# Mixture-of-experts stage of a two-layer trunk: wider weight pieces, a third extra buffer, and another path for the emptier experts

## The chip, the cores and the metric

The kernel runs on one core of a Trainium2 chip, in one launch. The metric is the device time in microseconds (us), the median of several executions. Engines are named as the profile names them: PE is TensorE, PEld its weight load, DVE VectorE, ACT ScalarE, POOL GpSimd, SP SyncE (here it only issues DMAs).

## What is computed

The trunk has two layers on 256 tokens of width 1024. The change touches the last stage alone, the expert layer of layer 1; in the reference it reads:

```
logits = (h @ router_w).astype(jnp.float32)
top_v, top_i = lax.top_k(logits, TOP_K)                 # 2 of 8 experts
gates = jax.nn.softmax(top_v, axis=-1)
combine = jnp.sum(jax.nn.one_hot(top_i, N_EXPERTS) * gates[..., None], axis=-2)
for e in range(N_EXPERTS):
    out = out + combine[..., e:e + 1] * swiglu(h, w13[e], w2[e])
# swiglu(h, w13, w2): a, b = split(h @ w13, 2);  (silu(a) * b) @ w2
x = x + g2 * out
```

w13 of one expert is 1024 x 5632 (twice 2816 columns), w2 is 2816 x 1024, all float32: 34.6 MB an expert, 276.8 MB for the eight.

## The kernel before

Tokens are brought together by expert. A place of 0 to 7 (called a rank here, r in the code) is an expert by number of tokens: place 0 is expert 0, the others stand in falling order of their counts, worked out on the chip (`plan`, inside `moe`). The order of work is `TURNS = (0, 1, 5, 2, 6, 3, 4, 7)`: ranks 0 to 4 are the big ones (up to 128 tokens each), ranks 5, 6 and 7 the small ones (up to 64). If an expert has more tokens than that, a second round runs under a branch; it does not run on these inputs.

For each rank, in this order:

- `gather` (L1588 to L1611): a 0/1 matrix Pt from the tokens' places (DVE, L1588), a product with the normed tokens xn (PE, L1602), scale and shift (ACT, L1607). xn is kept as two float32r parts (L1423, L1424), so each block takes four products. For a big rank DVE then splits xg into two parts (L1610, L1611).
- big ranks, `up_big`: w13 comes in chunks of 512 columns of each half. One weight tile (1 MB, a "raw" buffer) holds 4 blocks of 128 rows x 512 columns, so each contiguous piece is 2 KB; in the last chunk, of 256 columns, it is 1 KB. ACT makes the high part (L131) and DVE the low part (L132) of 1024 columns at a time, and PE does three float32r products for each block (L1643 to L1645), in the two "mm" PSUM banks. The result h is transposed (L150) and split (ACT L1656, DVE L1657). `down_big`: w2 in 11 tiles of 2 x 128 rows x 1024 columns (4 KB pieces), three products each (L1672 to L1674). `scatter_big`: gate, split, and two products for each half and token block against the places PT (L1684 to L1692).
- small ranks, `up` and `down`: plain float32, without a split, the tokens as two groups of 32 and the columns as four groups, so that four products of 32 columns of weights stand beside one another on PE (L1730, L1782). `CHUNKS` gives three chunks of the 2816 middle columns; the last is 4 x 192 wide, so that its middle blocks are 128 and 64 rows. Because of the 64-row blocks `down` takes the last rows of w2 by two DMAs of 64 partitions each (L1776), and the transposes of the last chunk have a 64-column form (L1747). The places are brought to four groups of 32 rows by 16 products (L1705). `scatter` gates all of y by one DVE instruction (L1796, with re-laid gates made once in `gate_groups`, L1533 and L1534), then runs 16 products of 32 rows (L1803) into four banks and 8 additions to x (L1808).

The scatter of a rank is held back as `tail` and issued in the first chunk of the next rank. The last rank (7) runs `down` and `scatter` on two halves of 512 columns, and each half is stored when it is done (L1524).

What sets the order: the kernel is recorded in program order, a scheduler then fixes the order of instructions on each engine at build time, and each engine runs its list in order. The raw buffers are used in turn: 5 + 4 + `R3` = 2, so 11. SP issues the next weight DMA when the buffer used 11 tiles ago is free: for a big rank when both split instructions have read it, for a small rank when PE has. There are four split tiles (high and low part of 1024 columns each), so splits stand at most four ahead of PE.

```
    CAPS = rounds.__func__((4, 4, 4, 4, 4, 2, 2, 2))
    TURNS = (0, 1, 5, 2, 6, 3, 4, 7)
    CHUNKS = ((0, 256), (1024, 256), (2048, 192))
```

Of the kernel before, what the change touches and what calls it, by code (L numbers as in the profile page):

```python
# [74 lines left out]
class Trunk:  # L75
# [1449 lines left out]

    def gate_groups(self):

        g = self.gates[(1, 1)]
        self.gateF = self.mp.tile([P, 256], F32, name="gateF")
        self.gateH = self.mp.tile([P, 2, P], F32, name="gateH")  # L1530
        for i in range(4):
            s = slice(32 * i, 32 * i + 32)
            self.nc.vector.tensor_copy(self.gateF[s, :], g[s, 256 * i:256 * i + 256])  # L1533
            self.nc.vector.tensor_copy(self.gateH[s], g[s].rearrange("p (h i c) -> p h i c", h=2, i=4)[:, :, i, :])  # L1534

    def experts(self, n, plan=None):
# [9 lines left out]
        xg, tail, got = self.gather(turns[0], caps, plan), None, None  # L1546
        for i, r in enumerate(turns):
            nt, hs, big = caps[r], [], r < self.BIG
            for c in range(-(-NF // 4) if big else len(self.CHUNKS)):
                with self.behind(self.lasts if i == 0 and c < 1 and plan else ()):  # L1550
                    if big:
                        self.up_big(r, c, xg[0], hs)
                    else:
                        self.up(r, c, nt, xg, hs)
                if c == 0 and tail:
                    tail()
# [5 lines left out]
            xg = self.gather(turns[i + 1], caps)  # L1562
            if big:
                tail = partial(self.scatter_big, r, self.down_big(r, hs), self.places_big(Pt))
            else:
                tail = partial(self.scatter, r, nt, self.down(r, nt, hs, 0, D), self.places(nt, Pt), 0, D)
# [4 lines left out]
        PT = self.places(nt, Pt)
        for h in range(2):
            self.scatter(r, nt, self.down(r, nt, hs, 512 * h, 512), PT, 512 * h, 512)
            self.store_x(slice(512 * h, 512 * h + 512))
# [259 lines left out]
```

## Time and profile before

| | us |
|---|---|
| median of 3 runs | 1432.94 (1431.07 to 1442.36) |
| the profiled execution | 1440.24 |
| its span | 1438.2 |
| expert stage in it: first gather product to end of span | 674.65 to 1438.2 |
| PE busy | 1365.4 (95%) |
| DVE busy | 988.5 (69%) |
| ACT busy | 715.5 (50%) |

Times in the rows below are microseconds from the span's start, and durations in "mean ns" are nanoseconds. A float32 product shows as two matmul records, a float32r product as one. Neighbouring records are pipelined, so a record's own duration is longer than the distance to the next; where PE is full, the distance is what counts. "x32" in a timeline row is a merged run of 32 records.

### The profile page before, as it was taken

The page shows a single profiled execution, that of the slowest core. Times are in us where ns is not written, and L with a number is a line of the kernel's source. Part 1 is how long each engine was busy: PE and PEld are TensorE (multiplying, and loading weights), DVE is VectorE, ACT ScalarE, POOL GpSimd, SP SyncE. Part 2 cuts the span into 40 slices and gives each one's busy share as a digit, 9 for nine tenths or more (in the row PEclk, how much of TensorE's full clock was granted, in tenths as well). Part 3 has the DMA queues.
Part 4 walks back from the last instruction along what each step waited for, and adds up shares of the span by engine and source line. Part 5 has one row for each costly group of instructions (what it writes and reads, how often), then busy time and mean ns, then how long its engine had stood idle before and what let it go on. Part 6 is the DMA issues. An engine that isn't in the chain of part 4 may idle for free.

```text
span 1438.2 us, 25509 instructions
## 1 busy us (share of the span) xinstructions
PE 1365.4 (95%) x10093; PEld 1057.9 (74%) x10093; DVE 988.5 (69%) x1646; ACT 715.5 (50%) x1107; POOL 121.7 (8%) x118
## 2 busy tenths in 40 slices
PE   3999999989999979999999999999999899999995
PEld 2877676789999968988888884367863578888545
DVE  6589767477888879656898984138951289898411
ACT  3553222364444355555778773036751268777410
POOL 3132321000000005320000000000000000000000
PEclk9799899999999989998999999999999999999998
DMA  9733343178888948507899998999999999999995
GB/s 268 240 117 118 118 134 103 59 263 264 292 266 292 320 156 264 178 29 266 296 366 333 355 344 284 382 351 386 397 384 397 349 387 396 388 364 345 339 372 186
DMA packets 226945, 400.90 MB, mean 279 GB/s; under 512 B 14861, under 2 KB 125954, under 8 KB 226818
## 3 DMA queue, kind: packets, MB, share of 16 engines
q1 hardware_dynamic: 220394, 398.00, 78.6%
q10 hardware_dynamic: 6424, 1.19, 0.5%
q8 instruction: 81, 1.33, 0.4%
q14 instruction: 46, 0.38, 0.1%
HBM read 398.11 MB, written 1.05 MB: 278 GB/s over the span
## 4 chain that ended last, share of the span: by engine, by line
PE 57%; DMA 3%; DVE 1%; issue 1%; ACT 1%; POOL 0%; SPq 0%; ACTq 0%; DVEq 0%
PE pab L1730 8%; PE pab L1644 7%; PE pab L1643 7%; PE pab L1645 7%; PE py L1673 4%; PE py L1672 4%; PE py L1674 4%; DMA raw<-in_odd_expert_w 3%; PE px L1602 2%; PE py L1782 2%; PE pth L150 1%; PE psc L1803 1%; PE pqk L398 1%; PE pqk L399 1%; PE pqk L400 1%
## 5 line engine op out<-in xcount | busy, mean ns | idle before, releaser
L131 ACT ACTIVATE whi<-raw 128x1024 fp32r<-128x1024 f32 (+1 forms) x472 | 484.5, 1037 | 305.0 <-PE pab L399 53.0
L132 DVE TENSOR_TENSOR wlo<-raw,whi 128x1024 fp32r<-128x1024 f32 (+1 forms) x472 | 560.5, 1207 | 103.7 <-ACT whi L131 100.6
L1644 PE MATMUL pab<-wlo,xg 128*128 128x512 f32 x440 | 175.1, 398 | 2.3 <-DVE wlo L132 2.3
L1645 PE MATMUL pab<-whi,xg 128*128 128x512 f32 x440 | 174.4, 396 | 0.0
L1643 PE MATMUL pab<-whi,xg 128*128 128x512 f32 x440 | 172.1, 401 | 1.5 <-ACT whi L131 1.5
L1730 PE MATMUL pab<-raw,xg 128*32 128x512 f32 (+1 forms) x1152 | 126.6, 559 | 0.0
L398 PE MATMUL pab<-hT,whi 128*128 128x256 f32 x352 | 101.4, 288 | 0.0
L399 PE MATMUL pab<-hT,whi 128*128 128x256 f32 x352 | 100.0, 284 | 0.6 <-DVE hT L388 0.3
L1644 PEld LDWEIGHTS pab<-wlo,xg 128*128 128x128 f32 x440 | 83.3, 189 | 22.6 <-DVE wlo L132 2.9
L1643 PEld LDWEIGHTS pab<-whi,xg 128*128 128x128 f32 x440 | 83.4, 190 | 22.1 <-ACT whi L131 2.4
L400 PE MATMUL pab<-hT,wlo 128*128 128x256 f32 x352 | 99.4, 283 | 0.0
L1645 PEld LDWEIGHTS pab<-whi,xg 128*128 128x128 f32 x440 | 83.2, 189 | 19.6 <-DVE xg L1611 0.5
L1730 PEld LDWEIGHTS pab<-raw,xg 128*32 128x32 f32 x1152 | 36.5, 110 | 72.3 <-issue 70.4
L282 DVE SCALAR_TENSOR_TENSOR adas<-raw,condr,adas 128x256 f32<-128x256 f32 x175 | 86.4, 499 | 3.1
L1673 PE MATMUL py<-wlo,hTe 128*128 128x512 f32 x220 | 88.3, 401 | 0.0
L1674 PE MATMUL py<-whi,hTe 128*128 128x512 f32 x220 | 86.6, 394 | 0.0
L1672 PE MATMUL py<-whi,hTe 128*128 128x512 f32 x220 | 74.1, 401 | 0.0
L1782 PE MATMUL py<-raw,hTe 128*32 128x256 f32 (+1 forms) x1408 | 65.4, 338 | 9.1 <-issue 6.3
L399 PEld LDWEIGHTS pab<-hT,whi 128*128 128x128 f32 x352 | 67.5, 192 | 1.7 <-DVE hT L388 1.4
L398 PEld LDWEIGHTS pab<-hT,whi 128*128 128x128 f32 x352 | 67.5, 192 | 0.3
L400 PEld LDWEIGHTS pab<-hT,wlo 128*128 128x128 f32 x352 | 67.4, 192 | 0.1
L1782 PEld LDWEIGHTS py<-raw,hTe 128*32 128x32 f32 x1408 | 45.2, 115 | 25.0 <-issue 11.1
(470 smaller groups left out, 2440.5 us busy)
## 6 DMA issues: line engine op xcount, KB each, us to landing
raw<-in_odd_expert_w SPq DMA_DIRECT2D x233, 1024.0 KB
raw<-in_ada_w SPq DMA_DIRECT2D x48, 1024.0 KB
raw<-in_even_ffn_w SPq DMA_DIRECT2D x33, 1024.0 KB
raw<-in_odd_expert_w SPq DMA_DIRECT2D x24, 768.0 KB
raw<-in_odd_w_qkv SPq DMA_DIRECT2D x12, 1024.0 KB
raw<-in_odd_expert_w SPq DMA_DIRECT2D x24, 512.0 KB
raw<-in_even_w_in SPq DMA_DIRECT2D x10, 1024.0 KB
raw<-in_even_w_out SPq DMA_DIRECT2D x4, 1024.0 KB
```

What stands on the lines that cost most here:

```text
L131: act = nc.scalar.activation(hs, src, AF.Copy)
L132: dve = nc.vector.tensor_tensor(l, src, hs, op=ALU.subtract)
L398: nc.tensor.matmul(out, wh[:, o:o + P], hT[:, k, 0, :], start=(k == 0), stop=False)
L399: nc.tensor.matmul(out, wh[:, o:o + P], hT[:, k, 1, :], start=False, stop=False)
L400: nc.tensor.matmul(out, wl[:, o:o + P], hT[:, k, 0, :], start=False, stop=(k == kd - 1))
L1643: PE.matmul(pab[-1], xg[:, k, 0, :], wh[:, o], start=(k == 0), stop=False)
L1644: PE.matmul(pab[-1], xg[:, k, 0, :], wl[:, o], start=False, stop=False)
L1645: PE.matmul(pab[-1], xg[:, k, 1, :], wh[:, o], start=False, stop=(k == KD - 1))
L1673: PE.matmul(py[n], hs[c][:, i, 0, :], wl[:, o], start=False, stop=False)
L1674: PE.matmul(py[n], hs[c][:, i, 1, :], wh[:, o], start=False, stop=(f == NF - 1))
L1730: PE.matmul(pu[t][32 * g:32 * g + 32, :2 * n].rearrange("p (x n) -> p x n", x=2), xg[0][:, k, 32 * t:32 * t + 32], v[:, :, g * n:(g + 1) * ...
L1782: PE.matmul(py[b][32 * g:32 * g + 32, o:o + n], hs[c][:, t, f, :], v[:, i, g * n:(g + 1) * n], start=(first and o == 0), stop=(last and (o ...
```

## The change

- `R3` 2 to 3: 12 raw buffers instead of 11.
- Big ranks: chunks of 1024, 1024 and 768 columns instead of 512. A weight tile is 2 blocks of 128 rows x 1024 (or 768) columns, so pieces are 4 KB (3 KB). A chunk's first half is summed in the two "mm" banks, its second half in two "gd" banks; both are evicted at the chunk's end.
- Small ranks: the last chunk's middle blocks are six whole blocks of 128 rows in the order of rows, so `down` reads 11 plain tiles of 128 partitions; the 64-row DMAs, the 64-column transposes and the DVE copies (L1755) go.
- Scatter: one function for all ranks. For a small rank eight DVE instructions of 32 rows bring the gated y from its 4 x 32 rows to 64 rows, ACT and DVE split it, and 8 float32r products of 64 rows with 512 columns replace the 16 of 32 rows with 256. The places are two transposes instead of 16 products. `gate_groups` goes.
- xn is one float32 tensor: the four DVE instructions of L1424 go, and `gather` takes two float32 products a block instead of four float32r ones.
- The tail stands in the middle of the next rank's first chunk; the last rank's first scatter is behind one more weight tile.

```
-    R3 = 2
+    R3 = 3
-        self.xn = mp.tile([P, NT, 2, D], F32R, name="xn")
+        self.xn = mp.tile([P, NT, D], F32, name="xn")
...
-    CHUNKS = ((0, 256), (1024, 256), (2048, 192))
+    CHUNKS = ((0, 1024), (1024, 1024), (2048, 768))
...  gather
-                        PE.matmul(px[:, kk * n:kk * n + n], self.xn[:, tt, h, k * P:(k + 1) * P], Pt[:, tt, :n],
+                    PE.matmul(px[:, kk * n:kk * n + n], self.xn[:, tt, k * P:(k + 1) * P], Pt[:, tt, :n], start=(tt == 0), stop=(tt == 1))
...  up_big
+        for x in range(2):
+            pab = [self.ps("gd" if x else "mm", "pab") for _ in banks]
+            for g in range(KD // 2):
+                v = self.raw(w13[g][:, :, x * F + c0:x * F + c0 + n], (2, n))
+                for i in range(2):
+                    k = 2 * g + i
+                    wh, wl = self.split(v[:, i, :], n)
+                    for p, (o, m) in zip(pab, banks):
+                        s = slice(o, o + m)
+                        PE.matmul(p[:, :m], xg[:, k, 0, :], wh[:, s], start=(k == 0), stop=False)
+                        PE.matmul(p[:, :m], xg[:, k, 0, :], wl[:, s], start=False, stop=False)
+                        PE.matmul(p[:, :m], xg[:, k, 1, :], wh[:, s], start=False, stop=(k == KD - 1))
+            if x == 0:
...
+                if tail:
+                    tail()
...  down (small ranks)
-        blocks.append(([(slice(64 * i, 64 * i + 64), w[P:, i::2]) for i in range(2)], [(2, 4), (2, 5)]))
+        w2 = self.weights("odd_expert_w2", r)[:, c0:c0 + cols].rearrange("(f p) n -> p f n", p=P)
...  scatter
+                for j in range(512 // q):
+                    g = 512 // q * n + j
+                    s = slice(32 * g, 32 * g + 32)
+                    for t in range(2):
+                        V.tensor_tensor(yf[32 * t:32 * t + 32, q * j:q * j + q], py[s, t],
+                                        gate[s, cs.start + q * j:cs.start + q * j + q], op=ALU.mult)
             S.activation(yh, yf, AF.Copy)
             V.tensor_tensor(yl, yf, yh, op=ALU.subtract)
             for tt in range(NT):
...
                 PE.matmul(px, PT[:, s], yh, start=True, stop=False)
                 PE.matmul(px, PT[:, s], yl, start=False, stop=True)
```

How the instructions move, at three places. First PE, at the seam from rank 5's `down` (py) to rank 2's `up_big` (pab); PT are rank 5's places, psc the scatter's sums. Before:

```order
L1782 MATMUL py_9500<-raw_9591,hTe_1715_9336 32x256 x16
L1705 MATMUL PT_9701<-cst,Pt_8836 32x128 x5
L1782 MATMUL py_9500<-raw_9609,hTe_1715_9336 32x256 x16
L1705 MATMUL PT_9701<-cst,Pt_8836 32x128 x8
L1782 MATMUL py_9500<-raw_9627,hTe_1715_9336 32x256 x16
L1705 MATMUL PT_9701<-cst,Pt_8836 32x128 x3
L1782 MATMUL py_9500<-raw_9645,hTe_1729_9431 32x256 x16
```

and the first of its scatter stands 34 rows behind the last of these, in the second half of rank 2's first chunk. The places PT now are two transposes of 64 columns, five `down` tiles ahead of the rows here. Now:

```order
L1742 MATMUL py_9532<-raw_9695,hTe_1751_9494 32x256 x16
L1742 MATMUL py_9532<-raw_9713,hTe_1751_9494 32x256 x16
L1637 MATMUL pab_9736<-whi_9740,xg_9499 128x512
L1637 MATMUL pab_9737<-whi_9740,xg_9499 128x512
L1638 MATMUL pab_9736<-wlo_9741,xg_9499 128x512
L1639 MATMUL pab_9736<-whi_9740,xg_9499 128x512
L1638 MATMUL pab_9737<-wlo_9741,xg_9499 128x512
L1639 MATMUL pab_9737<-whi_9740,xg_9499 128x512
L1637 MATMUL pab_9736<-whi_9750,xg_9499 128x512
L1637 MATMUL pab_9737<-whi_9750,xg_9499 128x512
L1769 MATMUL psc_9839<-yh_9831,PT_9731 128x512
L1769 MATMUL psc_9843<-yh_9831,PT_9731 128x512
```

The three runs of L1705 become one pair of transposes, and the scatter's first products move up to eight products behind the seam.

Second, DVE at the same seam: yf is rank 5's gated output, wlo the low parts of rank 2's first weights. Before:

```order
L1796 TENSOR_TENSOR yf_9820<-py_9500,gateF 128x512
L132 TENSOR_TENSOR wlo_9723<-raw_9720,whi_9722 128x1024
L132 TENSOR_TENSOR wlo_9733<-raw_9720,whi_9732 128x1024
L132 TENSOR_TENSOR wlo_9745<-raw_9742,whi_9744 128x1024
L132 TENSOR_TENSOR wlo_9755<-raw_9742,whi_9754 128x1024
L132 TENSOR_TENSOR wlo_9770<-raw_9767,whi_9769 128x1024
L132 TENSOR_TENSOR wlo_9780<-raw_9767,whi_9779 128x1024
```

Now:

```order
L1762 TENSOR_TENSOR yf_9830<-py_9532,gate_6054 32x256 x4
L132 TENSOR_TENSOR wlo_9741<-raw_9738,whi_9740 128x1024
L132 TENSOR_TENSOR wlo_9751<-raw_9738,whi_9750 128x1024
L1765 TENSOR_TENSOR yl_9832<-yf_9830,yh_9831 64x512
L132 TENSOR_TENSOR wlo_9763<-raw_9760,whi_9762 128x1024
L1762 TENSOR_TENSOR yf_9847<-py_9532,gate_6054 32x256 x4
L132 TENSOR_TENSOR wlo_9773<-raw_9760,whi_9772 128x1024
L132 TENSOR_TENSOR wlo_9785<-raw_9782,whi_9784 128x1024
L1771 SCALAR_TENSOR_TENSOR x<-psc_9839,combS,x 128x512
L1771 SCALAR_TENSOR_TENSOR x<-psc_9843,combS,x 128x512
L1765 TENSOR_TENSOR yl_9849<-yf_9847,yh_9848 64x512
```

The small rank's scatter, once one instruction in front of the splits and the rest far behind, now stands among the first five splits.

Third, SP, in rank 0's w13 (the tile's shape is partitions x blocks x columns). Before:

```order
L1637 DMA raw_7837<-in_odd_expert_w 128x4x512
L1637 DMA raw_7859<-in_odd_expert_w 128x4x512
L1637 DMA raw_7891<-in_odd_expert_w 128x4x256 x2
L1637 DMA raw_7914<-in_odd_expert_w 128x4x256 x2
L110 DMA raw_8000<-in_odd_expert_w 128x2x1024
```

Now:

```order
L110 DMA raw_7695<-in_odd_expert_w 128x2x1024
L110 DMA raw_7717<-in_odd_expert_w 128x2x1024
L110 DMA raw_7759<-in_odd_expert_w 128x2x768
L110 DMA raw_7781<-in_odd_expert_w 128x2x768
L110 DMA raw_7803<-in_odd_expert_w 128x2x768
```

The four narrow DMAs of the last chunk become eight of 768 columns, and the rest is 1024 columns wide.

## Rows read from the trace of the kernel before

**Rows 1.** The page's busy line, and its slices of the span (40 equal ones of 36 us; the expert stage begins in the 19th).

```profile
PE 1365.4 (95%) x10093; PEld 1057.9 (74%) x10093; DVE 988.5 (69%) x1646; ACT 715.5 (50%) x1107; POOL 121.7 (8%) x118
GB/s 268 240 117 118 118 134 103 59 263 264 292 266 292 320 156 264 178 29 266 296 366 333 355 344 284 382 351 386 397 384 397 349 387 396 388 364 345 339 372 186
```

**Rows 2.** Waits of PE from 674 us to the end, by what ended them (total us, times, longest).

```profile
PE py L1782 <- issue: 6.3, 4, 4.2
PE py L1782 <- DMA raw<-in_odd_expert_w: 2.7, 2, 2.5
PE pab L1644 <- DVE wlo L132: 2.3, 2, 1.5
PE pab L1643 <- ACT whi L131: 1.5, 1, 1.5
```

**Rows 3.** Windows: the stretch, its length, busy time (records) of PE, PEld, DVE, ACT, POOL, granted clock, DMA share, GB/s. In order: rank 3's w13 (2 KB pieces), rank 3's w2 (4 KB), rank 5's third chunk and its like in rank 6 (3 KB), the 64-partition DMAs of ranks 5 and 6.

```profile
1164.00:1184.00 20.00, 20.00 (x89) 15.83 (x88) 15.15 (x15) 14.07 (x16) 0.00 (x0) 1.00 1.05 387
1204.00:1224.00 20.00, 20.00 (x100) 16.58 (x99) 18.29 (x19) 15.97 (x21) 0.00 (x0) 1.00 1.03 409
1092.00:1104.00 12.00, 11.90 (x114) 3.48 (x106) 1.74 (x4) 0.77 (x2) 0.00 (x0) 1.00 1.03 400
948.00:956.00 8.00, 8.00 (x172) 5.64 (x168) 0.00 (x0) 0.00 (x0) 0.00 (x0) 1.00 1.03 204
1128.00:1136.00 8.00, 7.71 (x146) 4.43 (x140) 0.00 (x0) 0.00 (x0) 0.00 (x0) 1.00 1.04 231
```

**Rows 4.** Timeline of PE at the seam from rank 5 to rank 2, and of the first of the four parts of rank 5's scatter.

```profile
959.29 2.79 PE L1782 MATMUL py<-raw,hTe 128*32 128x256 f32 x47 [0.37 <-issue]
962.02 0.50 PE L1643 MATMUL pab<-whi,xg 128*128 128x512 f32 x1
964.02 0.51 PE L1644 MATMUL pab<-wlo,xg 128*128 128x512 f32 x1 [1.51 <-DVE wlo L132]
964.37 0.39 PE L1645 MATMUL pab<-whi,xg 128*128 128x512 f32 x1
964.60 0.39 PE L1643 MATMUL pab<-whi,xg 128*128 128x512 f32 x1
971.20 1.99 PE L1803 MATMUL psc<-yf,PTb 32*128 32x256 f32 x8
973.12 0.50 PE L1644 MATMUL pab<-wlo,xg 128*128 128x512 f32 x1
```

**Rows 5.** Timeline of DVE and ACT at the same seam and at the next one (rank 6 to rank 3).

```profile
962.14 0.69 DVE L1796 TENSOR_TENSOR yf<-py,gateF 128x512 f32<-128x512 f32 x1 [5.45 <-PE py L1782]
1142.57 2.00 ACT L131 ACTIVATE whi<-raw 128x1024 fp32r<-128x1024 f32 x2 [14.97 <-DMA raw<-in_odd_expert_w]
```

**Rows 6.** Groups by line and form from 674 us on: count, busy us, mean ns of one, idle before.

```profile
L132 DVE TENSOR_TENSOR wlo<-raw,whi 128x1024 fp32r<-128x1024 f32 x330 | 394.3, 1222 | 62.8 <-ACT whi L131 60.3 <-DMA raw<-in_odd_expert_w 0.5
L1657 DVE TENSOR_TENSOR hTe<-pth,hTe 128x512 fp32r<-128x512 f32 x25 | 17.1, 683 | 0.0
L1649 DVE TENSOR_TENSOR hb<-hb,pab 128x512 f32<-128x512 f32 x25 | 17.0, 680 | 0.5 <-PE pab L1645 0.5
L1692 DVE SCALAR_TENSOR_TENSOR x<-psc,combS,x 128x512 f32<-128x512 f32 x20 | 14.5, 748 | 19.9 <-PE psc L1691 19.6
L1796 DVE TENSOR_TENSOR yf<-py,gateH 128x256 f32<-128x256 f32 x2 | 0.8, 424 | 26.3 <-PE py L1782 26.3
L1808 DVE SCALAR_TENSOR_TENSOR x<-psc,combS,x 128x128 f32<-128x128 f32 x16 | 4.3, 345 | 2.5 <-PE psc L1803 2.5
L1686 DVE TENSOR_TENSOR yl<-yf,yh 128x512 fp32r<-128x512 f32 x10 | 6.9, 688 | 2.1 <-ACT yh L1685 2.1
L1685 ACT ACTIVATE yh<-yf 128x512 fp32r<-128x512 f32 x10 | 6.2, 622 | 25.0 <-DVE yf L1684 21.5 <-PE psc L1690 3.5
```

**Rows 7.** Timeline of DVE and PE at the start of the stage (router, places, first gather).

```profile
667.93 0.57 DVE L1533 COPY gateF<-gate 32x256 f32<-32x256 f32 x2
670.77 0.75 DVE L1424 SCALAR_TENSOR_TENSOR xn<-x,rs,xn 128x512 fp32r<-128x512 f32 x1
672.93 1.25 DVE L1424 SCALAR_TENSOR_TENSOR xn<-x,rs,xn 128x512 fp32r<-128x512 f32 x1
674.65 7.09 PE L1602 MATMUL px<-Pt,xn 128*128 128x128 f32 x32
```

**Rows 8.** Timeline of PE where rank 5's first chunk is woven into rank 1's w2.

```profile
871.89 1.04 PE L1730 MATMUL pab<-raw,xg 128*32 128x512 f32 x2
872.86 0.51 PE L1673 MATMUL py<-wlo,hTe 128*128 128x512 f32 x1
```

**Rows 9.** Timeline of PE and DVE in the last rank, from its last transposes to the last addition.

```profile
1395.11 0.44 PE L1747 MATMUL pth<-cst,hb 128*64 128x128 f32 x4
1395.48 1.08 PE L1705 MATMUL PT<-cst,Pt 128*32 128x128 f32 x32
1396.49 0.33 PE L150 MATMUL pth<-cst,hb 128*128 128x128 f32 x1
1397.12 5.66 PE L1782 MATMUL py<-raw,hTe 128*32 128x128 f32 x198
1428.38 0.42 DVE L1796 TENSOR_TENSOR yf<-py,gateH 128x256 f32<-128x256 f32 x1 [10.10 <-PE py L1782]
1430.05 2.16 DVE L1808 SCALAR_TENSOR_TENSOR x<-psc,combS,x 128x128 f32<-128x128 f32 x8 [1.25 <-PE psc L1803]
```

More of the change, by code (lines that the diff above doesn't have):

```diff
@@ L1524, in store_x @@
             self.nc.sync.dma_start(self.out[0, tt * P:(tt + 1) * P, cols], self.x[:, tt, cols])
[L1526 to L1534, printed above, removed]
     def experts(self, n, plan=None):
@@ L1545, in experts @@
             self.posS, self.combS, self.who = self.pos0, self.comb0, [0]
-        xg, tail, got = self.gather(turns[0], caps, plan), None, None
+        xg, tail, got = self.gather(turns[0]), None, None
         for i, r in enumerate(turns):
-            nt, hs, big = caps[r], [], r < self.BIG
-            for c in range(-(-NF // 4) if big else len(self.CHUNKS)):
+            hs, big = [], r < self.BIG
+            for c in range(len(self.CHUNKS)):
                 with self.behind(self.lasts if i == 0 and c < 1 and plan else ()):
[L1551 to L1556, printed above, removed]
+                    (self.up_big if big else self.up)(r, c, xg[0], hs, tail if c == 0 else None)
                 if c == 0 and i == 0 and plan:
@@ L1561, in experts @@
                 break
[L1562 to L1566, printed above, removed]
+            xg = self.gather(turns[i + 1])
+            py, steps = (self.down_big if big else self.down)(r, hs, 0, D)
+            for step in steps:
+                step()
+            tail = partial(self.scatter, r, py, self.places(r, Pt), 0, D)
+        PT = self.places(r, Pt)
         if big:
-            self.scatter_big(r, self.down_big(r, hs), self.places_big(Pt))
+            py, steps = self.down_big(r, hs, 0, D)
+            for step in steps:
+                step()
+            self.scatter(r, py, PT, 0, D)
             self.store_x(slice(0, D))
             return got
[L1571 to L1574, printed above, removed]
+        (py0, s0), (py1, s1) = (self.down(r, hs, c0, 512) for c0 in (0, 512))
+        for step in s0 + s1[:2]:
+            step()
+        self.scatter(r, py0, PT, 0, 512)
+        self.store_x(slice(0, 512))
+        for step in s1[2:]:
+            step()
+        self.scatter(r, py1, PT, 512, 512)
+        self.store_x(slice(512, D))
         return got
@@ L1578, in mtile, with gather @@
         return self.mp.tile(list(shape), dt, tag=name, name=self.nm(name), bufs=bufs)
-    def gather(self, r, caps, first=None):
+    def gather(self, r):
         self.mark(f"gather{r}")
@@ L1584, in gather @@
         big = r < self.BIG
-        n = P if big else 32 * caps[r]
-        Pt = tile("Pt", (P, NT, P), 2, F32R)
+        n = P if big else 64
+        Pt = tile("Pt", (P, NT, P), 2)
         for tt in range(NT):
@@ L1658, in up_big @@
-        hs.extend(hT[:, i:i + 2] for i in range(0, m, 2))
-    def down_big(self, r, hs):
-        self.mark(f"down{r}")
+        w13 = self.weights("odd_expert_w13", r).rearrange("(g k p) f -> g p k f", p=P, k=2)
+        c0, n = self.CHUNKS[c]
+        banks = [(o, min(512, n - o)) for o in range(0, n, 512)]
+        h = []
+        for x in range(2):
[11 more added lines that the diff above has]
+            if x == 0:
+                for p, (o, m) in zip(pab, banks):
+                    h.append(tile("hb", (P, 512), 3)[:, :m])
+                    S.activation(h[-1], p[:, :m], AF.Silu)
+                if tail:
+                    tail()
@@ L1664, in down_big, with step @@
         py = [self.ps("gd", "py") for _ in range(2)]
-        for c in range(NF // 2):
+        def step(c):
+            self.mark(f"down{r}")
             w2r = self.raw(w2[256 * c:256 * c + 256, :].rearrange("(k p) n -> p k n", p=P), (2, D))
```

285 lines of the change are left out of this document (111 added, 174 removed).

## The prediction

> **What bounds the kernel now.** I read the page's busy line and slices first, then the waits of PE, windows of the DMA stream, and last the timelines at the seams between ranks, since the change touches only the expert stage. PE is busy 95% of the span, VectorE 69% [rows 1]. From 674 us on the waits of PE name 6.3 us of issue, 2.7 of weights and 3.8 of splits, some 13 us in 764 [rows 2]. So the stage is PE's list of work plus a few holes, and the question is where a "busy" PE is slow. The windows answer half of it: in rank 3 PE is full for all 20 us at 387 GB/s and again at 409 GB/s, so inside a big rank a faster stream alone gives nothing [rows 3]. It pays where the stream is late: at 1128 us, on the 64-partition DMAs of rank 6, 231 GB/s arrive and PE begins to have holes, and ACT then waits for rank 3's first weights [rows 3, 5]. In the last rank PE takes 31.3 us (1397.12 to 1428.38) for 11 tiles of w2, where one run of 198 records takes 5.66, or 28.6 ns a record [rows 9]. All 704 records at that pace are 20.1 us, the first half's scatter about 0.9 more (32 records, an estimate at the same pace): some 10 us there go to the pace at which data land, though the trace calls PE busy.
>
> **The change, part by part.** The sum is made against the profiled execution, 1440.2 us, which lies 0.5% above the median of 1432.94; the gain is then taken from the median.
>
> 1. Start of the stage. Two gateF copies (0.57 together) and the low parts of xn (0.75 and 1.25) go from DVE's list ahead of the first gather at 674.65 [rows 7]. Together 2.6 us of DVE; ACT's part of xn and the router remain beside them, so not all is on the path. I take 2.0 (0 to 2.6). The gather itself costs PE the same: half the products, float32 instead of float32r, and so the same number of records.
>
> 2. Weaving. Rank 5's first products are put into rank 1's w2. A lone run of two records lasts 0.97 us (871.89 to 872.86) [rows 8]; with four products side by side the same two records cost a quarter, 0.24. The order has 8 lone runs instead of 11: at most 3 x 0.73 = 2.2, of which I take 1.5 (0 to 2.2), since the others carry as little company as before.
>
> 3. Places and narrow transposes. The 16 products for the places hold PE from 1395.48 to 1396.49, 1.01 us, and the 64-column transposes from 1395.11, 0.37 [rows 9]; the latter come twice in a rank. Instead come two transposes for the places (an estimate of 0.19, as two of the four in 0.37) and plain ones. That is about 1.01 - 0.19 + 2 x 0.37 - 0.1 = 1.5 a small rank, 4.5 for three (3 to 5).
>
> 4. Scatter of ranks 5 and 6. One of its four parts holds PE 1.92 us (971.20 to 973.12) [rows 4], so 7.7 in all. Now 8 products of 512 columns at the float32r distance, 0.23 (964.37 to 964.60) [rows 4], plus something for smaller edges: 2.0. PE saves 5.7. But VectorE is late next. At the seam to rank 2 PE already waits 1.51 us for the first low part, because yf (0.69) stands ahead of it [rows 4, 5]. Now four evictions of 32 rows stand there. The trace has none of 32x256; the nearest row is 0.424 for 128x256 [rows 6], bounded by that and, if fewer rows were cheaper, by half of it. At 0.42 they take 1.7, one more us than yf. Behind them, among the first five splits, come yl (0.69) twice, four more evictions and four additions of 0.75 [rows 6]: 7.8 us of VectorE work in all. A split is 1.22 there and six products of PE 1.40, so five splits absorb 0.9; PE's own scatter absorbs 1.9. PE then holds for about 5.0 where it held 1.5, 3.5 more at worst. I take 3.2: 2.5 a seam, 5.0 for both. If all of the 7.8 is exposed and the old work hidden, both together lose 8; if PE is given later splits ahead, they gain 12.
>
> 5. Waits for data. Rank 6's end: the 64-partition DMAs run at 204 to 231 GB/s where 4 KB pieces on 128 partitions have 409 [rows 3]; a stretch of 8 us then takes 4.0 to 4.5, about 4 us gained a pair, one pair in ranks 5 and 6 and two half-width ones in rank 7. A big rank's w13 (23.1 MB) takes 59.6 us at 387 and 56.4 at 409, 3.2 us less, and a 12th buffer lets the stream stand one tile more ahead (1.05 MB, 2.6 us). By 1142 the stream is ahead by more than the holes at the end of rank 6, 2.7 and 1.5 [rows 2, 5]: 4.2 gained. In rank 5, where PE has fewer records while 204 GB/s arrive, 2.0 as an estimate from half of one pair's 4. For rank 7 the two pairs and the 12th buffer make 4 + 2.6 and what rank 4 has over, as far as buffers allow; of the 10 I take 7.5. Together 13.7 (0, if the stream's lead is used up by buffers, to 20, if rank 7 runs at PE's own pace and rank 5 gives 6).
>
> A rule of the Trainium skill speaks against a part of this: "DMA: Bandwidth & Descriptors", section Specifications, gives line rate from 512 bytes upward, by which 2 KB pieces would lose nothing against 4 KB. The trace has 387 against 409 GB/s in the same rank [rows 3], so here the measurement decides; by the rule the 3.2 us of a big rank would not come, and with some 4 less for term 5 the sum would be about 20 instead of 24.
>
> 6. Tail. After the last product DVE gates 128x256 in 0.42 and adds to x until 1432.21, 3.8 us [rows 9]. Now eight instructions of 32x128; the nearest rows are 0.345 for 128x128 and 0.42 for 128x256 [rows 6], I take 0.30 for a smaller tile, so 2.4, then the high part 0.62, the low part 0.69, the products and two additions of 0.75 [rows 6]: 6.2. That is -2.4 (-3.5 at 0.42 and with nothing beside it, 0 if ACT and DVE overlap by blocks).
>
> At nothing I cost: the big ranks' products (the same columns, the same 396 x 0.23 us); SP's list (24 DMAs for w13 of a big rank before and after, 12 to 11 for a small one's w2); and the chunks' ends. These come in pairs now, two gatings of 0.680 and two low parts of 0.683 [rows 6], 2.7 us of DVE without a split. What hides them is that splits can stand four tiles ahead, 4 x 1.22 = 4.9 us. Without that cover a big rank has three such ends.
>
> The sum: 2.0 + 1.5 + 4.5 + 5.0 + 13.7 - 2.4 = 24.3. The profiled execution would be 1415.9, the median 1408.6, rounded 1408.5.
>
> **The rivals.**
>
> A, the savings turn into waits. If the small ranks are paced by their data throughout, what PE no longer has to do in them (terms 2 and 3) becomes waiting, and if the stream's lead is spent where the buffers are full, term 5 is nothing: 2.0 + 5.0 - 2.4, about 5, so 1428. For it speaks that the stream runs at 349 to 397 GB/s in every slice from 900 to 1260 us [rows 1]; against it, that PE in rank 5's third chunk is full at 400 GB/s [rows 3].
>
> B, the chunks' ends come through, the case on the other side. VectorE has 1.22 a split where PE needs 1.40 for its six products [rows 4, 6]; over the 16 splits of a chunk it gains 16 x 0.18 = 2.8 us and must spend 2.7 at the end. If it comes to the end without a lead, each of the 15 ends (three in five ranks) costs PE up to 2.7, 41 in all: 1432.9 - 24.3 + 41 = 1450. It decides from 24.3/15 = 1.6 us an end upward. Against it: DVE idled 60 us before its splits for ACT's high parts and PE's full list [rows 6], so it mostly stood at the limit of the four tiles; before, each end took half as much and left no wait of PE behind but the 2.3 of the seams [rows 2].
>
> C, the full gain. The seams hold PE no longer than before (DVE is fed by buffers earlier, or small tiles cost half), so term 4 is 11.4, and term 5 goes to 18: 2.0 + 1.5 + 4.5 + 11.4 + 18 - 2.4 = 35, so 1398. For it speaks that the stream, once ahead, has all first tiles of a rank waiting; against it, the order, which has the small rank's scatter on DVE between the splits.
>
> **How the numbers follow.** Chances: forecast 0.55, C 0.24, A 0.16, B 0.05. The forecast's own spread, with terms 1, 4, 5 and 6 at one bound or other by turns, is about 8 either way, 1400 to 1417. The range goes to C's far end (2.6, 2.2, 5, 12, 20 and 0 by the terms' upper bounds, 41.8 together, 1391) and to A with a little over: 1388 to 1430. What it leaves out is B and the outer parts of A and C, under 2 in 10. About 1% (14 us) is what a measurement of this kernel can tell from no change: faster is below 1418.6, which the forecast and C reach, 0.79; A lies within, 0.16; B is slower, 0.05.
>
> **What would show it.** In the profile after: the first gather at about 672.7; the small scatter's products near 2 us a rank; waits of PE for DVE's low parts at the seams to ranks 2 and 3 of about 5 us each (near 1.5 means C); 409 GB/s in the w13 stretches of ranks 2 and 3 and no stretch near 200; no PE hole at the end of rank 6 and rank 7's 11 tiles in about 24 us instead of 31; from the last down product to the span's end about 12 us instead of 9.8 (1428.4 to 1438.2). Wrong it would be if PE waits for low parts at every chunk's end (B), or if the issue and data waits of ranks 6 and 7 are as long as before (A).

## The result, and the profile after

The changed kernel takes 1420.24 us (median of 4 runs, 1415.69 to 1422.87) against 1433.43 for the kernel before: a ratio of 0.9893 (95% interval 0.9844 to 0.9943), 13 us less where 24.3 were forecast. The direction and the range held; the size was half, and the time stays above the 1418.6 that the prediction took for clearly faster. Its profiled span is 1420.9 us, 17.3 less than before, of which 3.3 was there before the expert stage: the product of L717 that begins at 631.89 in the one profile begins at 628.62 in the other, and the change touches none of that work. So the stage gave 14.0.

The busy line and the slices, as [rows 1]:

```profile
PE 1346.5 (95%) x10190; PEld 1051.9 (74%) x10190; DVE 990.9 (70%) x1665; ACT 718.8 (51%) x1134; POOL 121.9 (9%) x118
GB/s 267 247 119 120 120 159 80 60 273 261 296 267 296 310 147 276 197 31 221 338 357 386 282 393 306 392 408 404 382 354 390 408 406 398 366 271 398 344 385 174
```

The stream is faster, with slices up to 408 GB/s. The waits of PE in the stage, as [rows 2]:

```profile
PE pab L1638 <- DVE wlo L132: 4.8, 2, 2.4
PE psc L1769 <- ACT yh L1764: 4.7, 2, 3.2
PE py L1742 <- issue: 4.0, 2, 2.5
PE py L1671 <- DVE wlo L132: 1.4, 3, 0.5
```

The weight waits (2.7) and ACT's 1.5 are gone; the wait for low parts has doubled to two of 2.4 us. Both are at seams from a small rank to a big one. The 4.7 for ACT's yh are in the last rank's two scatters (1.46 and 3.25). PE's and DVE's timelines at the first, as [rows 4, 5]:

```profile
948.25 0.73 PE L1637 MATMUL pab<-whi,xg 128*128 128x512 f32 x2
951.39 0.50 PE L1638 MATMUL pab<-wlo,xg 128*128 128x512 f32 x1 [2.41 <-DVE wlo L132]
951.74 0.39 PE L1639 MATMUL pab<-whi,xg 128*128 128x512 f32 x1
951.97 0.39 PE L1638 MATMUL pab<-wlo,xg 128*128 128x512 f32 x1
...
954.99 0.63 PE L1639 MATMUL pab<-whi,xg 128*128 128x512 f32 x1
955.41 0.63 PE L1638 MATMUL pab<-wlo,xg 128*128 128x512 f32 x1
955.84 0.63 PE L1639 MATMUL pab<-whi,xg 128*128 128x512 f32 x1
...
948.39 1.70 DVE L1762 TENSOR_TENSOR yf<-py,gate 32x256 f32<-32x256 f32 x4 [8.38 <-PE py L1742]
950.11 2.36 DVE L132 TENSOR_TENSOR wlo<-raw,whi 128x1024 fp32r<-128x1024 f32 x2
954.23 1.73 DVE L1762 TENSOR_TENSOR yf<-py,gate 32x256 f32<-32x256 f32 x4
```

The four evictions take 1.70 us, as forecast (1.7). PE stands 2.41, 0.9 more than before and half of the 5.0 that the prediction gave as its sign. What it did not have at all: at 951.7 products are 0.23 us apart, at 955 they are 0.42. The windows have the granted clock third from the end (length; busy time and records of PE, PEld, DVE, ACT, POOL; clock; DMA share; GB/s):

```profile
948.00:952.00 4.00, 1.59 (x13) 0.81 (x6) 3.54 (x6) 1.88 (x3) 0.00 (x0) 1.00 1.03 408
952.00:956.00 4.00, 4.00 (x11) 2.35 (x10) 3.90 (x8) 1.69 (x2) 0.00 (x0) 0.58 1.02 409
956.00:960.00 4.00, 4.00 (x10) 2.31 (x9) 3.97 (x5) 1.58 (x2) 0.00 (x0) 0.50 1.03 410
960.00:964.00 4.00, 4.00 (x13) 3.12 (x12) 2.75 (x3) 2.01 (x2) 0.00 (x0) 0.64 1.03 410
964.00:968.00 4.00, 4.00 (x17) 2.76 (x16) 3.42 (x4) 2.02 (x3) 0.00 (x0) 1.00 1.02 410
```

After PE had stood still it was granted 1.2 GHz instead of 2.4 for some 10 us, about 5 us of work lost (by the windows 0.42, 0.50 and 0.36 of 4 us each, 5.1 in all). It is "100% busy" there, with 10 records in 4 us instead of 17. The seam to rank 3 looks the same (0.76, 0.50, 0.50 and 0.96 from 1128 to 1144). Before, the 1.51 us of [rows 4] were followed by 0.23 us steps. The tail, as [rows 9]:

```profile
1408.81 2.38 DVE L1762 TENSOR_TENSOR yf<-py,gate 32x128 f32<-32x128 f32 x8 [6.85 <-PE py L1742]
1411.30 0.63 ACT L1764 ACTIVATE yh<-yf 64x512 fp32r<-64x512 f32 x1 [12.06 <-DVE yf L1762]
1411.98 0.73 PE L1769 MATMUL psc<-yh,PT 64*128 64x512 f32 x2 [3.25 <-ACT yh L1764]
1413.24 1.41 DVE L1771 SCALAR_TENSOR_TENSOR x<-psc,combS,x 128x512 f32<-128x512 f32 x2 [0.59 <-PE psc L1770]
```

The last w2 product (py) ends at 1408.74, 12.2 us before the end of the span; before it was 9.9.

The stage by intervals between PE's first products (us; r2 is rank 2, "up" its first w13 product, "down" its first w2 product, "end" the last w2 product), read off PE's timeline in every run:

| run | first gather to r1 up | r1 down to r2 up | r2 up to down | r2 down to r3 up | r3 up to r4 up | r4 down to end | tail |
|---|---|---|---|---|---|---|---|
| before | 107.2 | 115.1 | 72.7 | 109.0 | 106.9 | 112.6 | 9.9 |
| after | 104.6 | 109.6 | 73.7 | 103.8 | 110.1 | 107.8 | 12.2 |
| c_after | 104.6 | 109.6 | 73.6 | 103.8 | 110.1 | 108.3 | 11.7 |
| e_fill | 105.1 | 109.6 | 69.5 | 103.2 | 104.7 | 109.7 | 12.0 |
| e_seam | 105.1 | 109.6 | 66.7 | 103.2 | 102.0 | 108.6 | 12.0 |
| e_oldsc | 105.3 | 112.9 | 65.7 | 106.8 | 100.6 | 109.4 | 10.0 |
| e_2kb | 104.6 | 109.6 | 70.4 | 103.8 | 111.4 | 108.2 | 11.7 |
| e_narrow | 104.5 | 110.0 | 73.3 | 107.5 | 104.1 | 111.3 | 12.2 |
| e_r3_2 | 104.6 | 109.2 | 70.4 | 104.0 | 105.6 | 109.1 | 13.2 |
| e_best | 105.3 | 109.6 | 66.8 | 103.1 | 102.0 | 109.6 | 10.0 |
| e_oldseam | 105.3 | 110.0 | 67.8 | 103.9 | 104.4 | 108.0 | 9.8 |
| e_seam_narrow | 104.6 | 109.6 | 68.0 | 107.9 | 104.0 | 112.3 | 12.5 |
| e_seam_r2 | 104.7 | 109.2 | 67.1 | 103.1 | 103.4 | 108.5 | 13.4 |

r1 and r4 "up to down" are 65.1 to 66.1 in every run.

### The profile page after: what moved, and what is told of

It reads as the page before. It is cut to its first block, busy times and chain, and to the rows that moved or that the text cites. A ratio compares the mean times of both kernels' runs of the same rounds, so it can differ in the third digit from the quotient of the medians.

```text
span 1420.9 us, 25760 instructions
## 1 busy us (share of the span) xinstructions
PE 1346.5 (95%) x10190; PEld 1051.9 (74%) x10190; DVE 990.9 (70%) x1665; ACT 718.8 (51%) x1134; POOL 121.9 (9%) x118
## 4 chain that ended last, share of the span: by engine, by line
PE 58%; DVE 3%; DMA 1%; issue 1%; ACT 1%; POOL 0%; ACTq 0%; DVEq 0%
PE pab L1694 8%; PE pab L1638 7%; PE pab L1637 7%; PE pab L1639 7%; PE py L1742 4%; PE py L1671 4%; PE py L1672 4%; PE py L1670 4%; PE px L1588 2%; PE pth L150 1%; PE pqk L398 1%; PE pqk L399 1%; PE pqk L400 1%; DVE wlo L132 1%; DMA raw<-in_odd_expert_w 1%
## 5 line engine op out<-in xcount | busy, mean ns | idle before, releaser
L131 ACT ACTIVATE whi<-raw 128x1024 fp32r<-128x1024 f32 (+2 forms) x492 | 486.2, 1004 | 307.3 <-PE pab L1639 57.5
L132 DVE TENSOR_TENSOR wlo<-raw,whi 128x1024 fp32r<-128x1024 f32 (+2 forms) x492 | 561.3, 1168 | 89.7 <-ACT whi L131 87.3
L1638 PE MATMUL pab<-wlo,xg 128*128 128x512 f32 x480 | 185.4, 387 | 4.8 <-DVE wlo L132 4.8
L1639 PE MATMUL pab<-whi,xg 128*128 128x512 f32 x480 | 179.2, 381 | 0.0
L1637 PE MATMUL pab<-whi,xg 128*128 128x512 f32 x480 | 141.4, 382 | 0.3 <-DVE xg L1595 0.3
L1694 PE MATMUL pab<-raw,xg 128*32 128x512 f32 (+1 forms) x1152 | 118.4, 523 | 0.0
L1638 PEld LDWEIGHTS pab<-wlo,xg 128*128 128x128 f32 x480 | 91.8, 191 | 29.9 <-DVE wlo L132 8.7
L1639 PEld LDWEIGHTS pab<-whi,xg 128*128 128x128 f32 x480 | 92.0, 192 | 17.3
L1637 PEld LDWEIGHTS pab<-whi,xg 128*128 128x128 f32 x480 | 86.1, 191 | 16.8 <-issue 1.2
L1714 DVE TENSOR_TENSOR hb<-hb,pab 128x256 f32<-128x256 f32 (+1 forms) x21 | 7.4, 363 | 87.7 <-ACT hb L1713 87.3
L399 PEld LDWEIGHTS pab<-hT,whi 128*128 128x128 f32 x352 | 67.8, 193 | 1.0 <-DVE hT L388 0.8
L1742 PE MATMUL py<-raw,hTe 128*32 128x256 f32 (+1 forms) x1408 | 60.5, 326 | 4.0 <-issue 4.0
```

The source lines that it names most:

```text
L131: act = nc.scalar.activation(hs, src, AF.Copy)
L132: dve = nc.vector.tensor_tensor(l, src, hs, op=ALU.subtract)
L399: nc.tensor.matmul(out, wh[:, o:o + P], hT[:, k, 1, :], start=False, stop=False)
L1637: PE.matmul(p[:, :m], xg[:, k, 0, :], wh[:, s], start=(k == 0), stop=False)
L1638: PE.matmul(p[:, :m], xg[:, k, 0, :], wl[:, s], start=False, stop=False)
L1639: PE.matmul(p[:, :m], xg[:, k, 1, :], wh[:, s], start=False, stop=(k == KD - 1))
```

## The experiments

The kernel before took 1435.8 us (median) beside c_after, e_fill, e_seam and e_oldsc, 1439.0 beside e_2kb, e_narrow, e_r3_2 and e_best, and 1437.0 beside e_oldseam, e_seam_narrow and e_seam_r2. Each ratio is against its own, so runs of different sets are compared by ratio and by the intervals of the table. The profile is of one execution.

**c_after, the control.** 

> The changed kernel again, beside the others on one chip. All theories: 1420 us as before, with a PE wait of about 2.4 us at the seams to ranks 2 and 3 and a granted clock of 0.50 for some 10 us behind each.

1419.41 us, ratio 0.9879 (0.9855 to 0.9904), with the same two waits of 2.4 us and the same stretches at 0.50.

**e_fill, work in place of the wait.**

```
+ if x == 0 and k == 0 and tail and tail.args[0] >= self.BIG:
+     for _ in range(10):
+         PE.matmul(pab[0][:, :512], xg[:, k, 0, :], wh[:, :512], start=True, stop=True)
```

> Ten products that nothing uses are put on PE at the start of ranks 2 and 3 (2.3 us each), where it waits for the first low part; VectorE's list is as in the changed kernel. Theory 1 (PE's idle stretch at the seam is followed by a granted clock of 0.50, and this is what eats the scatter's gain): no stretch at 0.50 behind the seams, PE only follows VectorE there, some 4 us won at each seam, about 1412 us although PE does more. Theory 2 (VectorE's longer list paces PE there, the clock is a side effect): products at full clock just wait for low parts, the same time as the changed kernel, 1419 to 1421. Theory 3 (the scatter gained as forecast, the shortfall is elsewhere): 1420 or up to 5 more for the added products.

1415.39 us, ratio 0.9857 (0.9832 to 0.9881). The interval overlaps the control's; the trace decides. PE's timeline has the ten products:

```profile
949.26 2.59 PE L1637 MATMUL pab<-whi,xg 128*128 128x512 f32 x10
```

and the windows behind it:

```profile
949.00:953.00 4.00, 3.91 (x23) 2.68 (x16) 3.53 (x6) 1.87 (x3) 0.00 (x0) 1.00 1.03 410
953.00:957.00 4.00, 4.00 (x16) 2.28 (x14) 3.90 (x7) 1.70 (x2) 0.00 (x0) 1.00 1.02 408
957.00:961.00 4.00, 4.00 (x18) 3.15 (x18) 3.96 (x5) 3.57 (x5) 0.00 (x0) 1.00 1.02 409
```

With ten products that nothing uses in the hole and VectorE's list unchanged the clock stays at 1.00, and the two intervals shrink by 4.1 and 5.4 us. More work on PE, less time: theory 1 holds and theory 2 falls. At a full clock VectorE's list holds PE nowhere else in these chunks: among the waits of PE that the profile lists for this run, none is of a w13 product for a low part.

**e_seam, the wait taken away.**

```
+ if x == 0 and k == 3:
+     spl = list(self.lastsplit)
...
- tail()
+ with self.behind(spl if tail.args[0] >= self.BIG else ()):
+     tail()
```

> The small rank's scatter is put behind the fourth split of the next big rank on VectorE and ScalarE; nothing else changes. Theory 1: PE does not stop at the seam, the clock stays at 1.00, 5 to 6 us won at each seam, about 1409 us. Theory 2: the 7.8 us of VectorE work come later as waits for low parts, less than 2 us won in all, 1418 to 1420. Theory 3: at most the 1.5 us by which the seam wait is longer, 1418 to 1420.

1408.17 us, ratio 0.9806 (0.9779 to 0.9834): 11.2 below the control. DVE splits ahead in the time in which it had idled, then gates (its timeline):

```profile
944.03 2.36 DVE L132 TENSOR_TENSOR wlo<-raw,whi 128x1024 fp32r<-128x1024 f32 x2 [4.19 <-ACT whi L131]
946.58 2.36 DVE L132 TENSOR_TENSOR wlo<-raw,whi 128x1024 fp32r<-128x1024 f32 x2 [0.19 <-ACT whi L131]
948.86 1.69 DVE L1765 TENSOR_TENSOR yf<-py,gate 32x256 f32<-32x256 f32 x4
```

The windows of the same seam:

```profile
948.00:952.00 4.00, 4.00 (x21) 3.21 (x18) 3.64 (x6) 1.89 (x2) 0.00 (x0) 1.00 1.03 410
952.00:956.00 4.00, 4.00 (x17) 2.76 (x16) 3.79 (x6) 2.77 (x4) 0.00 (x0) 1.00 1.02 410
```

PE waits nowhere for low parts in these chunks. So the 7.8 us of VectorE work did fit; only its place was wrong.

**e_oldsc, the old outputs path in the changed kernel** (`scatter`, `places` and `gate_groups` of the kernel before, for ranks 5 to 7).

```
- tail = partial(self.scatter, r, py, self.places(r, Pt), 0, D)
+ tail = partial(self.scatter_old, r, py, self.places_old(r, Pt), 0, D)   # small ranks
```

> The changed kernel with the old path of the small ranks' outputs: one gating instruction with re-laid gates, 16 float32 products of 32 rows, the places by 16 products. Theory 1: the seams wait 1.5 us without a fall of the clock, which gives back about what PE's scatter adds (5.7 a seam), the places cost 1.0 each and the tail is 2.4 shorter: 1416 to 1420, no slower than the changed kernel. Theory 2: the same, 1416 to 1420, but without a stretch of 0.50 having been needed for it. Theory 3: 2 x 2.5 + 3 x 1.0 - 2.4 = 5.6 us slower than the changed kernel, about 1426.

1413.21 us, ratio 0.9840 (0.9815 to 0.9865), 6.2 below the control: as built, the new path cost time. Theory 3 is out, and theories 1 and 2, which both gave 1416 to 1420, are not told apart here. The old path does not stand where it stood before, though: the first half of the scatter is ahead of the next rank's first product, so that PE waits 0.9 us there and not 1.5, and some 3 us move from the intervals "r2 up to down" and "r3 up to r4 up" into the ones ahead of them. One more thing shows: the same 16 products of 32 rows cost PE less than before, in PE's timeline at the second seam:

```profile
1122.98 2.00 PE L1556 MATMUL psc<-yf,yl 32*128 32x256 f32 x16 [0.91 <-DVE yf L1550]
1139.52 2.96 PE L1556 MATMUL psc<-yf,yl 32*128 32x256 f32 x16
```

The first sixteen records, of two row groups in turn, take 2.00 us, the others, one group behind the other, 2.96; in [rows 4] eight records of one group take 1.99. (The row groups are read from the program, where each has eight such records; the trace shows the two paces.) That is 5.0 us a scatter instead of 7.7: part of what I credited to the new shape was the old order's.

**e_oldseam, the old path behind the fourth split** (both edits above).

> The old path of the small ranks' outputs (one gating instruction, 16 products of 32 rows, places by 16 products) behind the fourth split of the next rank, so that neither path meets the wait at the seam. Theory 1 (without the wait the new scatter is the cheaper one on PE, by about 2 us a seam with its places): 2 to 3 us a seam more than the new scatter in the same place, the tail 2 us less, about 1410 us against 1408. Theory 2 (the new scatter's saving on PE came from the order of the old one, which stood in four runs of one row group): no more than 1 us a seam, and with the shorter tail 1406 us or less.

1412.50 us, ratio 0.9823 (0.9808 to 0.9838). Against e_seam the four intervals from r1 down to r4 up are 0.4, 1.1, 0.7 and 2.4 longer, 4.6 in all, of which two sets of places are 2.0 by [rows 9], and the tail 2.2 shorter. That is theory 1 in its sum, but the new scatter itself is worth little over 1 us a seam, not 5.7. Even that holds some 1.6 us of a fall of the clock in rank 3 (0.59 from 1144 to 1148, the last section); without it, half a microsecond a seam is left. The two ratios' intervals overlap, so this is read from one profile each.

**e_2kb, pieces of 2 KB again.**

```
- v = self.raw(w13[g][:, :, x * F + c0:x * F + c0 + n], (2, n))
+ v = self.rawtile()[:, :2 * n].rearrange("p (a k m) -> p a k m", a=2, k=2)
+ for a in range(2):
+     o = x * F + c0 + a * (n // 2)
+     nc.sync.dma_start(v[:, a], w13[g][:, :, o:o + n // 2])
```

> The changed kernel (1419 us), with each w13 tile of a big rank brought by two DMAs of half its columns: pieces of 2 KB (1.5 KB in the last chunk) as in the kernel before, the rest as changed. Theory 1 (the faster stream is worth what term 5 says of it): the stream falls from 409 to about 390 GB/s in the w13 stretches, 3 us a rank, and the ends of ranks 6 and 7 come 3 to 7 us later, 1422 to 1426 us. Theory 2 (in big ranks the stream waits for buffers, and its lead at rank 6's end does not come from the pieces): within 1 us of the changed kernel.

1416.41 us, ratio 0.9853 (0.9830 to 0.9876): not slower. The ends of ranks 6 and 7 move by 0.0 and 0.4 us at most; theory 2. And the same wait of 2.4 us has another price, in the windows at the first and second seam:

```profile
951.00:955.00 4.00, 4.00 (x13) 2.50 (x12) 3.90 (x8) 1.64 (x2) 0.00 (x0) 0.72 1.05 387
955.00:959.00 4.00, 4.00 (x17) 2.75 (x16) 3.97 (x5) 2.89 (x4) 0.00 (x0) 1.00 1.05 388
...
1128.00:1132.00 4.00, 4.00 (x10) 2.32 (x8) 3.40 (x5) 1.38 (x2) 0.00 (x0) 0.50 1.05 387
1132.00:1136.00 4.00, 4.00 (x10) 2.81 (x9) 3.37 (x5) 1.25 (x2) 0.00 (x0) 0.50 1.05 387
```

The stream does run at 387 GB/s here, but the first stretch at 1.2 GHz is some 3 us long and the second over 13, after equal waits (2.42). So rank 2 is 3.2 us shorter than in the control and rank 3 1.3 longer. The rest of the 3.5 us between the two profiled spans is mostly ahead of the stage (1.5), and the ratios' intervals overlap: this run is not shown to be faster.

**e_narrow, 64-partition DMAs again.**

```
+ v = self.rawtile()[:, :m * cols].rearrange("p (k n) -> p k n", n=cols)   # last tile
+ for o in (0, 64):
+     self.nc.sync.dma_start(v[o:o + 64], w2[o:o + 64, f0:f0 + m])
```

> The changed kernel with the last w2 tile of each small rank (the last of each half in rank 7) brought by two DMAs of 64 partitions. Theory 1: these run near 204 GB/s and cost the stream 2.5 us a tile of rank 5 and 6 and about 1.3 a half in rank 7; PE waits for them at the end of ranks 6 and 7, 3 to 6 us in all, 1422 to 1426 us. Theory 2 (the stream has enough lead now): only rank 7's last one shows, 1 to 2 us, 1420 to 1421.

1421.49 us, ratio 0.9880 (0.9857 to 0.9904), the control's: by the time alone nothing was lost, as in theory 2. The intervals say otherwise: ranks 6 and 7 end 3.7 and 3.1 to 3.5 us later, and rank 3 is 6.0 faster. PE's timeline around the seam to rank 3:

```profile
1127.00 1.93 PE L1747 MATMUL py<-raw,hTe 128*32 128x256 f32 x32 [1.03 <-DMA raw<-in_odd_expert_w]
1130.30 0.73 PE L1637 MATMUL pab<-whi,xg 128*128 128x512 f32 x2 [1.36 <-ACT whi L131]
1132.01 0.50 PE L1638 MATMUL pab<-wlo,xg 128*128 128x512 f32 x1 [0.98 <-DVE wlo L132]
```

and in the windows:

```profile
1130.00:1134.00 4.00, 2.73 (x10) 1.64 (x10) 3.96 (x6) 3.72 (x5) 0.00 (x0) 1.00 1.02 406
1134.00:1138.00 4.00, 4.00 (x16) 2.50 (x15) 3.90 (x7) 2.97 (x4) 0.00 (x0) 1.00 1.03 410
```

PE idled in three pieces with work between them, and the clock stayed: the loss was paid back at the seam. (At the first seam a wait of 2.05 us was followed by 0.50 as before.)

**e_seam_narrow, the same without the seam.** 

> The kernel of 1408 us (small scatter behind the fourth split) with the last w2 tile of each small rank by two DMAs of 64 partitions. Theory 1 (the narrow DMAs cost the waits that the trace showed, 3.7 us at rank 6's end and 3.5 at rank 7's, hidden in the changed kernel's time by a seam that then kept its clock): 1415 us. Theory 2 (the stream has the lead to hide them, so the time did not move): 1408 to 1410.

1419.37 us, ratio 0.9875 (0.9857 to 0.9893): 10 us above e_seam, 4.7 at rank 6's end, 3.7 at rank 7's, and 1.2 and 2.0 in ranks 2 and 3. Theory 1, with more than I gave it. Part of that is again the clock: at rank 6's end 32 records behind a wait of 2.51 us take 2.82 us and not 1.93, with 0.57 granted, so the narrow DMAs themselves cost some 3.8 there, as in e_narrow; in rank 7, 128 records behind a wait of 3.65 take 6.23 and not 3.70.

**e_r3_2 and e_seam_r2, 11 buffers** (`R3 = 2`, in the changed kernel and in e_seam). 

> The changed kernel with 11 raw buffers instead of 12. Theory 1 (the buffer's tile of lead, 2.6 us, is used where PE waits for data): 2 to 3 us slower, at the end of rank 7 above all, 1421 to 1423 us. Theory 2 (the lead is not what binds): within 1 us of 1419.

> The kernel of 1408 us with 11 raw buffers. Theory 1 (the 12th buffer is worth the 1.2 us that rank 7's w2 took longer without it, and the 4 us won in the changed kernel without it were a shorter stretch at the lower clock): 1409 to 1410 us. Theory 2 (11 buffers are the better number in themselves): 1404.

1415.08 us, ratio 0.9840 (0.9818 to 0.9863), and 1412.04, ratio 0.9811 (0.9791 to 0.9832). Without the 12th buffer the changed kernel is 4 us faster or a little more (the ratios' intervals, 0.9840 against 0.9879, just touch). Its stretches at the lower clock are short, and ranks 2 and 3 take 3.2 and 4.5 us less than in the control. In the windows behind the first seam:

```profile
948.00:952.00 4.00, 4.00 (x11) 2.53 (x12) 3.93 (x7) 2.12 (x3) 0.00 (x0) 0.65 1.02 408
952.00:956.00 4.00, 4.00 (x17) 2.78 (x16) 3.94 (x5) 2.64 (x3) 0.00 (x0) 1.00 1.02 409
```

Without the seam's wait the two numbers of buffers cannot be told apart (0.9811 against 0.9806); the 1404 us of theory 2 are out. The profiles have rank 7's end 1.2 us later in the one pair and 0.2 earlier in the other, and tails 1.0 and 1.4 longer. But rank 7's end does not measure the buffer. In it PE has a hole of 2.78 us in the control and in e_r3_2 alike; the records behind it, the control's first:

```profile
1395.18 3.47 PE L1742 MATMUL py<-raw,hTe 128*32 128x128 f32 x117 [2.78 <-issue]
1383.56 5.14 PE L1742 MATMUL py<-raw,hTe 128*32 128x128 f32 x116 [2.78 <-issue]
```

The same records take 1.7 us more in e_r3_2, where 0.57 was granted from 1384 to 1388; the control has 1.00 from 1396 to 1400. In the other pair the fall, again 0.57, is in e_seam alone. What the tile of lead is worth stays open; no profile shows more than some 2 us.

**e_best, the tail repaired too** (e_seam with the old path in rank 7). 

> The scatter of ranks 5 and 6 behind the fourth split of the next rank, as in the run that had 1408 us, and the last rank with the old scatter (one gating instruction, 16 products of 32 rows, the places by 16 products). Theory 1 (the eight gatings of 32x128 and the split are what made the tail 2.4 us longer): from the last down product to the end 9.9 us instead of 12.2, less 1.0 for the places, 1406 to 1407 us. Theory 2 (what ends the span is the store of x): 1408, the tail as long as before.

1407.94 us, ratio 0.9786 (0.9760 to 0.9812), the fastest beside e_seam; the intervals of the two overlap. The tail is 10.0 us, 2.0 less than in e_seam, and rank 7's end 1.0 later with its places: theory 1, by the profile. DVE in the tail:

```profile
1394.99 0.42 DVE L1550 TENSOR_TENSOR yf<-py,gateH 128x256 f32<-128x256 f32 x1 [4.32 <-PE py L1788]
1396.66 2.16 DVE L1561 SCALAR_TENSOR_TENSOR x<-psc,combS,x 128x128 f32<-128x128 f32 x8 [1.25 <-PE psc L1556]
```

## Why the prediction came out at half

Gains by the table above, beside the forecast's terms:

| stretch | forecast | measured |
|---|---|---|
| start, term 1 | 2.0 | 2.6 (gather 5.8 earlier, 3.3 of it older) + 2.6 |
| rank 1's w2 and rank 5 (terms 2, 3, 5) | 1.5 + 1.5 + 2.0 | 5.5 |
| seams and scatter, rank 2 and rank 3 (term 4) | 5.0 | -1.0 and -3.2 |
| end of rank 6 (terms 3, 5) | 1.5 + 4.2 | 5.2 |
| rank 7 (terms 3, 5) | 1.5 + 7.5 | 4.8 |
| tail (term 6) | -2.4 | -2.3 |

- **Term 4 failed**, by 9.2 us, most of the 10 that are missing (the start's 3.2 more and rank 7's 4.2 less nearly cancel). Its working named the order and the longer eviction (1.7, measured 1.70), but its price of a seam, "PE then holds for about 5.0 where it held 1.5", is wrong twice over. The wait is 2.41, not 5.0; and behind it comes a clock of 1.2 GHz for some 10 us, 5.1 us of lost work, which the term had at nothing and which e_fill and e_seam take away. So the loss that came (0.9 of wait, 5.1 of clock) is not the hold that was forecast (3.5 more than before). PE's saving was wrong too, even against the old order: in e_seam a pair of the new products delays PE by some 0.75 us (from 953.77 to 954.99 stand two products of 0.23 and a pair), four pairs by 3.0 and not 2.0, so 4.7 are saved of 7.7, not 5.7; and of the 7.7, 2.7 were their order in the list (e_oldsc), so that in equal places the new scatter is worth little over 1 us a seam at most (e_oldseam). With these sizes rank 2 closes: 4.7 - 0.9 - 5.1 = -1.3, measured -1.0. Rank 3 is left with about 1 us more loss than they give.
- **VectorE does not lack 5 us** at the seam: e_fill has the same VectorE list and PE follows it behind the first low part, and e_seam has the same VectorE work and no wait for it at all. VectorE had idled 8.38 us before the seam, time that the balance did not count.
- **Term 5**: for ranks 5 and 6 about the right sum (with terms 2 and 3, 10.7 measured and 10.7 forecast), but from one of its causes alone. The 64-partition DMAs carry it (e_narrow, e_seam_narrow: 3.7 and some 3.8 at rank 6's end). The 4 KB pieces gave at most 0.4 us (e_2kb). Rank 7 was given 7.5 and has 3 to 4: its w2 takes 27.1 us (1381.67 to 1408.74), not about 24, the stream runs at 382 to 390 GB/s from 1380 to 1396, and PE still waits there, 4.0 us by the page's word "issue".
- **Rank 7's "pace at which data land"** was misread as well. Of those 10 us of the kernel before the trace calls 5.9 idle and not busy (holes of 4.25, 1.37 and 0.32, called issue), which may well be data. But behind the longest hole the clock fell; here is that run of records and a window in it:

```profile
1407.02 7.39 PE L1782 MATMUL py<-raw,hTe 128*32 128x128 f32 x154 [4.25 <-issue]
1408.00:1412.00 4.00, 4.00 (x84) 3.61 (x80) 0.00 (x0) 0.00 (x0) 0.00 (x0) 0.50 1.05 387
```

At 0.50 there are 84 records in 4 us, 48 ns a record and not 28.6. So what cost the seams could be seen before the change. Rank 7 has 1.00 throughout its w2 in the changed kernel; how much of its gain is the clock's and how much the data's no run separates.
- **Terms 2, 3 and 6**: 2 and 3 are only seen in sums with term 5; the places alone are about 1.0 in rank 7 (e_best; the term has 1.01 - 0.19). Term 6 came out (-2.3; -1.8 in the control). Term 1's 2.0 is in order. The further 2.6 us up to rank 1 go with the first gather, 7.09 us long in [rows 7] at 0.50 and partly at full clock after. The clock there is not the change's alone: 0.66 and 0.91 were granted from 668 to 676 after, 0.50 and 0.79 in e_seam, whose code is the same up to there and whose interval is 0.5 longer. No experiment separates the two.
- **Rival A** was right that pieces of 4 KB are worth nothing, but the savings did not turn into waits: terms 2, 3 and the 64-partition part of 5 came. Its time, 1428, lies outside the runs (1415.69 to 1422.87), and so does the forecast's 1408.6; the measured 1420.24 is even nearer to A. That the sum fell between them is no merit of either. **B** did not happen: r1 and r4 take the same 65 us from up to down as before, so the paired chunk ends are covered. **C** gave a wait near 1.5 us as its sign, and 2.41 is nearer to that than to 5.0; its gain still did not come, as neither C nor the forecast had a price for the clock.

What stays open: why stretches at 1.2 GHz after waits of 2.0 to 2.4 us last some 3 us in one place and 10 to 14 in another, and why none follows in others. The length of a single idle stretch does not settle it: a hole of 2.78 us was followed by 1.00 in c_after and by 0.57 in e_r3_2. And the kernel before had these waits at its seam to rank 3, and 1.00 in every window from 1128 to 1156 (the last line is one):

```profile
1140.25 1.93 PE L1782 MATMUL py<-raw,hTe 128*32 128x256 f32 x32 [2.45 <-DMA raw<-in_odd_expert_w]
1143.68 0.50 PE L1643 MATMUL pab<-whi,xg 128*128 128x512 f32 x1 [1.50 <-ACT whi L131]
1144.94 0.50 PE L1644 MATMUL pab<-wlo,xg 128*128 128x512 f32 x1 [0.76 <-DVE wlo L132]
1144.00:1148.00 4.00, 3.24 (x14) 2.51 (x14) 3.63 (x4) 2.59 (x3) 0.00 (x0) 1.00 1.05 388
```

That the seams' loss is the clock's is shown by e_fill and e_seam; when the clock falls is not.

## What to carry to other kernels

When an evictor's list puts the evictions of one stage ahead of the operand preparation of the next, the price may be more than the wait: look behind every idle stretch of PE for records that are twice as far apart while PE reads 100% busy. Place such work behind the first few preparations, so that the evictor's idle time before the seam is used. An edit can then seem worth nothing, or 4 us, merely because it breaks up that idle stretch or changes how long the clock stays down behind it (e_narrow, e_r3_2), so read the stage's intervals and the clock before the total.
